# Norm rows behind the first FFN blocks, and a down projection with its load order written by hand

## The chip, the cores and the metric

The kernel runs on one core of a Trainium2 chip. The engines of the core work in parallel, each through its own instruction stream in order: TensorE (PE in the profile: matrix products into PSUM), VectorE (DVE), ScalarE (ACT), GpSimd (POOL) and SyncE (SP), which here does nothing but issue DMA transfers. They wait for each other through semaphores. The metric is the time of one execution on the device in microseconds. Before the change it is 1984.14 us, the median of three runs (1983.55 to 1985.42).

## The reference

One layer of a hybrid decoder for a prompt of 1024 tokens and 8 sample requests of 4 tokens each, so NT = 1056 tokens. Every sub-layer has a residual sum and an RMS norm ahead of it: a mixer (a gated MLP along the chunks beside a multi-head latent attention with a paged cache), a cross attention into a memory, and a convolutional FFN. Only the end of it matters here:

```python
o = einsum('nhtm,nmhd->nthd', p, mv); y = o @ w_mo          # memory cross-attention, out projection
x = x + y
h = rms_norm(x, g_ffn)                                      # x * rsqrt(mean(x*x) + eps) * g
gate, val = split(h @ w_up)                                 # 1024 -> 2 x 2816
conv = b_conv + sum(gpad[:, j:j+t] * w_conv[j] for j in range(3))
out = x + (silu(conv) * val) @ w_down                       # 2816 -> 1024
```

All is in 32-bit floating point with the precision that goes with it.

## The kernel before

Features lie on the 128 partitions and tokens along the free dimension. The 1056 tokens are two halves of HT = 528, each two columns of QT = 264. The 2816 features of the FFN are NF = 22 tiles of 128.

**Products.** Each operand is split into a rounded part hi and a rest lo (`split`, L186: ScalarE casts hi at L190, VectorE subtracts to lo at L191), and each product is three matmuls, hi by hi, hi by lo and lo by hi (`mm3`, L178 to L184). All products of the kernel therefore carry line 184 in the profile, and go by the names of what they write. A weight is loaded into `raw` (three buffers), and split into `hi` and `lo` (three buffers each); `stream` (L1302) does this for one tile of up to 8 blocks of 128 x 128.

**The memory attention's end** (`mem_attention`, L1524). `out` makes the output product in PSUM tiles named b, s and t in turn. VectorE adds each to the residual `res` (L1702), ScalarE multiplies by the gain into `y` (L1704) and squares for the norm (L1520), and GpSimd sums the squares into `ya`, the tile `acc` (L1521). `operands` (L1767) makes from y the seven operands of the FFN's blocks for each half (b11, b21, b22, t1, t3, t2, t4; sums by VectorE at L1775, splits at L190 and L191). The half's number is in the names: b110h is the hi part of b11 of half 0. The norm factor itself is not multiplied into the operands. `half_norm` (L1738) sums `ya` over the partitions by five matmuls and takes the inverse root in some dozen small VectorE operations (rqx, rqh, rqy, rqa, hr: L219 to L230). `half_row` (L1748) turns the 528 factors into a tile with the same row on each partition: five diagonal tiles by VectorE (`diag`, L1757), five matmuls with ones (sx, st: L1758), two copies by ScalarE (`row`, L1759). Both are called in the attention, ahead of the FFN, for half 0 and for half 1.

**The up projection** (`ffn_up`, L1830). Eleven pairs of feature tiles; for each pair four blocks: gate of half 0, gate of half 1, value of half 0, value of half 1. A `block` (L1843) is a 2 x 2 product by Winograd's form of Strassen's scheme, seven products in place of eight, in 84 matmuls: A (12), X twice (12 each), F (24), E (24), with sums by VectorE in between (a, z, zz) and results in G (gate) or C (value). The gate is multiplied by `row` (L1886), goes through the convolution (`cv`, L1893 to L1905), SiLU (L1906) and once more `row` (by GpSimd, L1907). The value block's C is multiplied in (L1923), and ScalarE's queue stores the result, the activation, in DRAM (`actd`, L1925). `weights` (L1794) makes the weights' sums on GpSimd (s12, s34: L1814 to L1818) and their splits.

**The down projection** (`ffn_down`, L1941). For each half it loads 22 activations (`araw`, a ring of four, L1952), splits them (`ah`, `al`, 27 buffers each), and for each of 8 output tiles m streams three weight tiles `w_down` of 8, 8 and 6 blocks and makes two columns `d` of 66 matmuls each. VectorE adds the residual (`yres`, loaded at L1967, added at L1968) and SP stores the output (`o_y`, L1969).

**Order.** The order of instructions on each engine is not that of the code: a scheduler with a timeline model of the chip orders them all, and adds the waits. Buffers come from pools with a fixed number per name; a tile waits until the last readers of the buffer's earlier tile are done. A pool that is opened where a closed one lay waits in the same way for that one's tiles. Only inside a manual section the named engines keep the order of the code.

Of the kernel before, what the change touches and what calls it, by code (L numbers as in the profile page):

```python
# [13 lines left out]
P = 128  # L14
# [8 lines left out]
FF, NF = 2816, 22  # L23

HT, QT = 528, 264
# [128 lines left out]
class Net:  # L154
# [1369 lines left out]
    def mem_attention(self, xh, xl, r3):  # L1524
        nc, tc, I, O = self.nc, self.tc, self.I, self.O
# [22 lines left out]
        w, st = {}, {}  # L1548
# [127 lines left out]
        self.pw, self.nw = self.open("pw", side="right"), 0  # L1676
        pc = self.open("pc", side="right")
        y1 = [self.t(pc, [P, 2, 2, HT], F32, f"y{d}") for d in range(2)]
        acc = self.t(pc, [P, 640], F32, "ya")
        pc0 = self.open("pc0", side="right")  # L1680
        nc.gpsimd.memset(acc[:, HT:], 0.0)

# [53 lines left out]
        return ops, rows, first  # L1736

    def half_norm(self, p, pp, acc):  # L1738

        nc = self.nc  # L1740
        st = self.t(pp, [P, 512], F32, "st", 1)
# [6 lines left out]
    def half_row(self, p, pp, r, row):  # L1748

        nc = self.nc  # L1750
        for a, z, tag in ((0, 4, "sx"), (4, 5, "st")):
            ps = self.t(pp, [P, 512], F32, tag, 1)
            n = min(HT, z * P) - a * P
            for i in range(a, z):
                w = min(P, HT - i * P)
                dg = self.t(p, [P, P], F32, "diag", 2)[:w, :w]
                nc.vector.tensor_scalar(dg, self.ident[:w, :w], r[:w, i : i + 1], None, ALU.mult)  # L1757
                nc.tensor.matmul(ps[:, (i - a) * P : (i - a) * P + w], self.ones[:w], dg, start=True, stop=True)  # L1758
            nc.scalar.copy(row[:, a * P : a * P + n], ps[:, :n])  # L1759
# [63 lines left out]
        w["a22"] = hi, lo  # L1823
        return w

    def ffn(self, ops, rows, w):
        self.ffn_up(ops, rows, w)
        self.ffn_down()

    def ffn_up(self, ops, rows, first):  # L1830

        nc, I, O = self.nc, self.I, self.O
        p = self.open("pf")
# [33 lines left out]
        def gate(w, fs, h, prev):  # L1867
# [73 lines left out]
    def ffn_down(self):  # L1941

        nc, I, O = self.nc, self.I, self.O
        p = self.open("pd", side="right")
        pp = self.open("psd", space=PSUM)
        parts = ((0, 8), (8, 16), (16, 22))
        for h in range(2):
            o = h * HT
            act = []
            for k in range(NF):  # L1950
                raw = self.t(p, [P, HT], F32, "araw", 4)
                nc.sync.dma_start(raw, self.act_dram[:, k, o : o + HT])  # L1952
                hi, lo = (self.t(p, [P, HT], FR, x, 27) for x in ("ah", "al"))
                self.split(hi, lo, raw)
                act.append((hi, lo))
            for m in range(8):
                ps = [self.t(pp, [P, 512], F32, "d", 6)[:, :QT] for c in range(2)]
                for a, z in parts:
                    w = self.stream(I["w_down"][m, :, a:z], z - a)
                    for c in range(2):  # L1960
                        t = slice(c * QT, c * QT + QT)
                        self.mm3(ps[c], [(w[0][:, k], w[1][:, k]) for k in range(z - a)],
                                 [(act[k][0][:, t], act[k][1][:, t]) for k in range(a, z)], first=a == 0, last=z == NF)
                for c in range(2):
                    t = slice(o + c * QT, o + c * QT + QT)
                    res = self.t(p, [P, QT], F32, "yres", 4)
                    nc.sync.dma_start(res, self.y_dram[:, m, t])  # L1967
                    nc.vector.tensor_tensor(res, ps[c], res, ALU.add)  # L1968
                    nc.sync.dma_start(O["o_y"][m, :, t], res)  # L1969
        self.close("psd")  # L1970
        self.close("pd")


def build(tc, I, O, stop=99, tap=None):
# [35 lines left out]
        N.close(x)  # L2010
    if done(5):
        return
    ops, rows, w = N.mem_attention(xh, xl, r3)
    if done(6):
        return
    N.ffn(ops, rows, w)
    for name in reversed(list(N.pools)):
        N.close(name)

# [30 lines left out]
```

## Time and profile before

| what | value |
|---|---|
| median of three runs | 1984.14 us |
| profiled execution | 1984.73 us |
| its span, first to last instruction | 1983.0 us |
| mean granted TensorE clock | 0.978 of full |
| TensorE busy | 1881.5 us, 95% |
| VectorE, ScalarE, GpSimd busy | 1363.9, 899.7, 707.1 us |
| first and last product of the up projection | 1256.25 and 1705.5 us |
| last product of the down projection | 1979.2 us |

The profile is that of one execution. Its page gives each engine's busy time, a chain of work that ended last (followed back from the last instruction, at each step to what released it), the costliest groups of instructions, and the DMA issues with their median time from issue to landing. Answers of the trace give single instructions with start and duration, what an engine waited for, and tables by stretches of time. PE means matmuls, SPq and ACTq the queues on which SP and ScalarE issue transfers. "x24" is a count.

### The profile page before, as it was taken

The numbers are of one execution on the slowest core, as the hardware profiler recorded it, in microseconds if no ns is written. First come the engines' busy times: TensorE is split into PE (matmuls) and PEld (weight loads), VectorE is DVE, ScalarE is ACT, GpSimd is POOL, SyncE is SP. The second block draws the span as 40 slices with busy tenths as digits, with TensorE's granted clock in tenths as the row PEclk, the third lists the DMA queues.
The fourth block names the chain that finished last, engine by engine and source line by source line (L and its number), as shares of the span: only waits on it lengthen the run. The fifth ranks groups of instructions, "written<-read, shape, count | busy, mean of one in ns | idle before, by whom it ended". The sixth has DMA issues, their size and how long they took to land.

```text
span 1983.0 us, 40178 instructions
## 1 busy us (share of the span) xinstructions
PE 1881.5 (95%) x14556; PEld 1768.9 (89%) x14556; DVE 1363.9 (69%) x2988; ACT 899.7 (45%) x1878; POOL 707.1 (36%) x811
## 2 busy tenths in 40 slices
PE   6999799999999999999999987799999999899999
PEld 5999777768898899888899976799999999899999
DVE  7865867766777766776645659788888888642521
ACT  6334676665555555555432546333333323331411
POOL 5231402003544444444032026377677776100000
PEclk9999899999999999999999999799999999899999
DMA  5101100207765566653653065022222222664642
GB/s 200 50 5 60 45 1 1 74 2 205 214 178 172 157 178 178 177 168 128 187 171 130 22 210 161 22 87 81 82 69 74 86 91 72 183 193 124 201 126 65
DMA packets 130312, 229.42 MB, mean 116 GB/s; under 512 B 20449, under 2 KB 86850, under 8 KB 130114
## 3 DMA queue, kind: packets, MB, share of 16 engines
q1 hardware_dynamic: 122914, 213.91, 36.1%
q10 hardware_dynamic: 7200, 12.95, 1.7%
q8 instruction: 115, 1.88, 0.4%
q14 instruction: 83, 0.68, 0.1%
HBM read 195.13 MB, written 31.66 MB: 114 GB/s over the span
## 4 chain that ended last, share of the span: by engine, by line
PE 69%; DVE 9%; issue 4%; DMA 3%; POOL 1%; ACT 1%; SPq 0%; POOLq 0%; DVEq 0%; ACTq 0%
PE s L184 15%; PE d L184 12%; PE b L184 7%; PE X L184 6%; PE F L184 6%; PE E L184 6%; PE A L184 3%; PE o L847 2%; PE tp L834 2%; DMA araw<-actd 1%; PE tp L184 1%; PE o L1277 1%; DVE mx L1228 1%; PE tp L789 1%; DVE y L1775 1%
## 5 line engine op out<-in xcount | busy, mean ns | idle before, releaser
L184 PE MATMUL s<-w2h,ch 128*128 128x288 f32 (+1 forms) x1024 | 306.7, 299 | 0.0
L184 PE MATMUL s<-w2h,cl 128*128 128x288 f32 (+1 forms) x1024 | 295.6, 289 | 2.1 <-POOL cl L1164 1.3
L184 PE MATMUL s<-w2l,ch 128*128 128x288 f32 (+1 forms) x1024 | 295.4, 288 | 0.0
L184 PEld LDWEIGHTS s<-w2h,ch 128*128 128x128 f32 x1024 | 193.3, 189 | 19.1 <-issue 13.6
L184 PE MATMUL d<-ah,hi 128*128 128x264 f32 x704 | 200.7, 288 | 9.0 <-ACT ah L190 9.0
L184 PE MATMUL d<-al,hi 128*128 128x264 f32 x704 | 201.2, 287 | 0.0
L184 PE MATMUL d<-ah,lo 128*128 128x264 f32 x704 | 201.2, 287 | 0.0
L184 PEld LDWEIGHTS s<-w2h,cl 128*128 128x128 f32 x1024 | 193.1, 189 | 2.8 <-POOL cl L1164 1.6
L184 PEld LDWEIGHTS s<-w2l,ch 128*128 128x128 f32 x1024 | 193.5, 189 | 0.0
L1207 DVE TENSOR_REDUCE ss<-sq 128x16 f32<-128x1024 f32 x128 | 155.4, 1214 | 50.0 <-ACT sq L1204 49.8
L191 DVE TENSOR_TENSOR lo<-raw,hi 128x1024 fp32r<-128x1024 f32 (+1 forms) x71 | 82.8, 1169 | 134.8 <-ACT hi L190 134.8
L190 ACT CAST hi<-raw 128x1024 fp32r<-128x1024 f32 (+1 forms) x71 | 70.9, 999 | 184.7 <-PE d L184 152.8
L1164 POOL TENSOR_TENSOR cl<-cT,ch 128x512 fp32r<-128x512 f32 x64 | 83.5, 1304 | 170.3 <-ACT ch L1160 151.5
L184 PEld LDWEIGHTS d<-ah,hi 128*128 128x128 f32 x704 | 133.9, 191 | 9.9 <-ACT ah L190 9.9
L184 PEld LDWEIGHTS d<-al,hi 128*128 128x128 f32 x704 | 134.3, 191 | 0.5 <-DVE al L191 0.5
L184 PEld LDWEIGHTS d<-ah,lo 128*128 128x128 f32 x704 | 134.1, 191 | 0.0
L1204 ACT ACTIVATE sq<-s 128x512 f32<-128x512 f32 x128 | 76.5, 598 | 92.2 <-PE s L184 92.2
L1201 ACT ACTIVATE sq<-s 128x512 f32<-128x512 f32 x128 | 76.6, 599 | 85.3 <-PE s L184 85.0
L184 PE MATMUL mm<-whi,xh 128*128 128x256 f32 (+3 forms) x288 | 84.7, 296 | 12.7 <-ACT xh L194 11.2
L184 PE MATMUL mm<-whi,xl 128*128 128x256 f32 (+3 forms) x288 | 82.6, 298 | 6.5 <-DVE xl L197 6.4
L1521 POOL TENSOR_TENSOR acc<-acc,sqx 128x384 f32<-128x384 f32 (+1 forms) x42 | 46.2, 1101 | 111.7 <-ACT sqx L1520 110.7
L184 PE MATMUL mm<-wlo,xh 128*128 128x256 f32 (+3 forms) x288 | 84.3, 294 | 0.0
(672 smaller groups left out, 6316.8 us busy)
## 6 DMA issues: line engine op xcount, KB each, us to landing
cT<-cT SPq DMA_DIRECT2D x256, 160.0 KB, 2.6
ck<-ck SPq DMA_DIRECT2D x256, 144.0 KB, 3.2
raw<-w_up SPq DMA_DIRECT2D x44, 512.0 KB, 3.6
raw<-w_down SPq DMA_DIRECT2D x32, 512.0 KB, 3.8
actd<-cv ACTq DMA_DIRECT2D x44, 264.0 KB, 2.3
araw<-actd SPq DMA_DIRECT2D x44, 264.0 KB, 4.0
raw<-w_down SPq DMA_DIRECT2D x16, 384.0 KB, 3.2
res<-res SPq DMA_DIRECT2D x16, 264.0 KB, 2.8
```

The lines of the kernel that those rows point to most:

```text
L184: self.nc.tensor.matmul(out, l, r, start=first and i == 0, stop=last and i == len(seq) - 1)
L190: {"act": nc.scalar.copy, "pool": nc.gpsimd.tensor_copy, "dve": nc.vector.tensor_copy}[eng](hi, src)
L191: low = lambda: nc.vector.tensor_tensor(lo, src, hi, ALU.subtract)
L789: nc.tensor.transpose(tp[:, j * P : j * P + P], s[x, g * 4 + j][:, h % 4], self.ident)
L834: nc.tensor.transpose(tp[:, z * P : z * P + P], u[e][:, jj * P : jj * P + P], self.ident)
L847: nc.tensor.matmul(u["o"][jj * 64 : jj * 64 + 64, c], s["v"][:, j + jj, h % 4], th[:, jj * 256 : jj * 256 + c.stop - c.start], start=j == ...
L1164: (nc.vector if k else nc.gpsimd).tensor_tensor(d["l"][:, k], src[k], d["h"][:, k], ALU.subtract)
L1201: nc.scalar.activation(sq[:, 0], ps[:, :, n0 : n0 + 256], AF.Square)
L1204: nc.scalar.activation(sq[:, 1], pt.rearrange("p (e d) -> p e d", e=2), AF.Square)
L1207: yield lambda: nc.vector.tensor_reduce(s["ss"][:, g0 : g0 + 2].rearrange("p e (z h) -> p z e h", z=2), sq.rearrange("p z e (h d) -> p z e ...
L1228: nc.vector.tensor_reduce(s["m"][:, z], S[:, g0:g1].rearrange("p g m -> p m g"), AX.X, ALU.max)
L1521: nc.gpsimd.tensor_tensor(acc, acc, sq, ALU.add)
```

## The change

There are three parts. The norms move: `ya`, the norm factors and the diagonal tiles lie in the pool `pw`, which stays open through the FFN, and `half_norm` and `half_row` take their PSUM from the caller. Half 0's `half_norm` stays in the attention; its row, and half 1's norm and row, are made in `ffn_up` behind the first gate block of the half, with PSUM from the ring "A" of the blocks. The value's C shares the ring of two buffers of G. And `ffn_down` is written anew: hi and lo of an activation share one tile "a" with 27 buffers, and 16 tiles that are never used are taken ahead of the first, so that the first eleven activations get buffers 16 to 26, which lie where half 0's operands b11 to t2 were, while the others follow from buffer 0 on. The order of SP is that of the code: four activations, the first three weight tiles, 18 activations, and then for each m two `yres`, the next m's weight tiles and the two stores of the m before; half 1's activations 0 to 4 follow the products of m = 6 of half 0, and 5 to 21 the stores that stand in half 1's m = 0.

```diff
-        acc = self.t(pc, [P, 640], F32, "ya")
+        acc = self.t(self.pw, [P, 640], F32, "ya")
...
-        norms = [self.half_norm(pc, pp, acc)]
+        norms = [self.half_norm(self.pw, self.t(pp, [P, 512], F32, "st", 1), acc)]
...
-        self.half_row(pc, pp, norms[0], rows[0])
...
-        self.half_row(pc, pp, self.half_norm(pc, pp, acc), rows[1])
...
+        def norm(h, new):
+            if h:
+                norms.append(self.half_norm(self.pw, new(), acc))
+            self.half_row(self.pw, new, norms[h], rows[h])
...
             block(w, ops[h], place)
+            if fs[0] == 0:
+                norm(h, lambda: self.t(pp, [P, 512], F32, "A", 2))
...
-            C = self.t(p, [P, 4 * QT], F32, "C")
+            C = self.t(p, [P, 2, HT + 2], F32, "G", 2).rearrange("p e n -> p (e n)")[:, : 4 * QT]
...
+        def raws(m):
+            out = []
+            for a, z in parts:
+                out.append(self.t(self.wr, [P, 8, P], F32, "raw")[:, : z - a])
+                nc.sync.dma_start(out[-1], I["w_down"][m, :, a:z])
+            return out
+        def acts(h, ks):
+            for k in ks:
                 raw = self.t(p, [P, HT], F32, "araw", 4)
+                nc.sync.dma_start(raw, self.act_dram[:, k, h * HT : h * HT + HT])
+                a = self.t(p, [P, 2, HT], FR, "a", 27)
+                self.split(a[:, 0], a[:, 1], raw)
+                act[h].append((a[:, 0], a[:, 1]))
+        def store(h, m, ps):
+            for c in range(2):
+                t = slice(h * HT + c * QT, h * HT + c * QT + QT)
+                nc.vector.tensor_tensor(res[h, m][c], ps[c], res[h, m][c], ALU.add)
+                nc.sync.dma_start(O["o_y"][m, :, t], res[h, m][c])
+        for _ in range(16):
+            self.t(p, [P, 2, HT], FR, "a", 27)
+        act, res = [[], []], {}
+        with self.tc.manual_schedule(engines={mybir.EngineType.SP}):
+            acts(0, range(4))
+            raw = raws(0)
+            acts(0, range(4, NF))
+            old = None
+            for h in range(2):
+                for m in range(8):
+                    res[h, m] = []
                     for c in range(2):
+                        res[h, m].append(self.t(p, [P, QT], F32, "yres", 4))
+                        nc.sync.dma_start(res[h, m][c], self.y_dram[:, m, h * HT + c * QT : h * HT + c * QT + QT])
+                    w = [self.stream(None, z - a, raw=r) for (a, z), r in zip(parts, raw)]
+                    if h + m < 8:
+                        raw = raws((m + 1) % 8)
+                    if old:
+                        store(*old)
+                    if (h, m) == (1, 0):
+                        acts(1, range(5, NF))
+                    ps = [self.t(pp, [P, 512], F32, "d", 6)[:, :QT] for c in range(2)]
+                    for (a, z), x in zip(parts, w):
+                        for c in range(2):
...
+                    if (h, m) == (0, 6):
+                        acts(1, range(5))
+                    old = h, m, ps
+            store(*old)
```

More of the change, by code (lines that the diff above doesn't have):

```diff
@@ L1732, in mem_attention, with half_norm @@
             self.operands(y1[d], d, ops[1], self.FORMS[3:])
-        self.half_row(pc, pp, self.half_norm(pc, pp, acc), rows[1])
         self.close("psa")
         self.close("pc")
-        return ops, rows, first
-    def half_norm(self, p, pp, acc):
+        def norm(h, new):
+            if h:
+                norms.append(self.half_norm(self.pw, new(), acc))
+            self.half_row(self.pw, new, norms[h], rows[h])
+        return ops, rows, norm, first
+    def half_norm(self, p, st, acc):
         nc = self.nc
-        st = self.t(pp, [P, 512], F32, "st", 1)
         for i in range(5):
@@ L1746, in half_norm, with half_row @@
         return r
-    def half_row(self, p, pp, r, row):
+    def half_row(self, p, new, r, row):
         nc = self.nc
-        for a, z, tag in ((0, 4, "sx"), (4, 5, "st")):
-            ps = self.t(pp, [P, 512], F32, tag, 1)
+        for a, z in ((0, 4), (4, 5)):
+            ps = new()
             n = min(HT, z * P) - a * P
@@ L1824, in weights, with ffn, ffn_up @@
         return w
-    def ffn(self, ops, rows, w):
-        self.ffn_up(ops, rows, w)
+    def ffn(self, *a):
+        self.ffn_up(*a)
         self.ffn_down()
-    def ffn_up(self, ops, rows, first):
+    def ffn_up(self, ops, rows, norm, first):
         nc, I, O = self.nc, self.I, self.O
@@ L1946, in ffn_down @@
         parts = ((0, 8), (8, 16), (16, 22))
[L1947 to L1950, printed above, removed]
-                raw = self.t(p, [P, HT], F32, "araw", 4)
[L1952 to L1959, printed above, removed]
-                    for c in range(2):
[L1961 to L1969, printed above, removed]
@@ new lines, in store @@
+        def store(h, m, ps):
[14 more added lines that the diff above has]
+                    res[h, m] = []
+                    for c in range(2):
+                        res[h, m].append(self.t(p, [P, QT], F32, "yres", 4))
[10 more added lines that the diff above has]
+                        for c in range(2):
+                            t = slice(c * QT, c * QT + QT)
+                            self.mm3(ps[c], [(x[0][:, k], x[1][:, k]) for k in range(z - a)],
+                                     [(act[h][k][0][:, t], act[h][k][1][:, t]) for k in range(a, z)], first=a == 0, last=z == NF)
+                    if (h, m) == (0, 6):
+                        acts(1, range(5))
+                    old = h, m, ps
+            store(*old)
@@ L2012, in build @@
         return
-    ops, rows, w = N.mem_attention(xh, xl, r3)
+    ffn = N.mem_attention(xh, xl, r3)
     if done(6):
         return
-    N.ffn(ops, rows, w)
+    N.ffn(*ffn)
     for name in reversed(list(N.pools)):
```

## The prediction

> **What bounds the kernel now.** I read the page's busy shares and chain first, then the chain of waits around the two places that the change touches, then the timelines of single engines there. TensorE is busy almost the whole span and heads the chain, so time can only come out of stretches in which it stands still or runs at half clock.
>
> ```profile
> PE 1881.5 (95%) x14556; PEld 1768.9 (89%) x14556; DVE 1363.9 (69%) x2988; ACT 899.7 (45%) x1878; POOL 707.1 (36%) x811
> PE 69%; DVE 9%; issue 4%; DMA 3%; POOL 1%; ACT 1%; SPq 0%; POOLq 0%; DVEq 0%; ACTq 0%
> ```
>
> The FFN's up projection has no such stretch: in its stage TensorE is busy 448.75 of 449.00 us at full clock (columns: busy time and count by engine, granted clock, DMA share, GB/s).
>
> ```profile
> 1256.00:1705.00 449.00, 448.75 (x3681) 448.75 (x3682) 374.50 (x480) 153.59 (x199) 301.46 (x230) 1.00 0.24 77
> ```
>
> The stretches lie before and behind it. The first, from the chain (start, duration, what):
>
> ```profile
> 1225.65 1.64 PE b L184 x11
> 1234.35 0.34 DVE res L1702
> 1234.69 3.21 DVE diag L1757 x2
> 1250.12 0.62 DVE t41l L191
> 1250.73 0.09 DVE rqy L222
> 1253.08 2.39 PE sx L1758 x8
> 1255.49 0.72 ACT row L1759 x2
> 1256.25 3.01 PE A L184 x12
> 1259.26 3.17 PE X L184 x24
> 1278.48 1.47 PE A L184 x12
> 1288.69 1.46 PE A L184 x12
> ```
>
> The last output product of the memory attention ends at 1227.3. VectorE then makes half 1's operands (to 1250.7) and the norm, and the first FFN matmul starts at 1256.25, at half clock (3.01 us for an A that takes 1.46 later). A block is 10.2 us (1278.48 to 1288.69). The second stretch is the change to the down projection:
>
> ```profile
> 1704.17 1.34 PE E L184 x11
> 1705.54 0.84 ACT hi L190
> 1706.40 0.97 DVE lo L191
> 1709.19 6.62 DMA araw<-actd
> 1722.73 2.74 DMA araw<-actd
> 1735.99 4.07 DMA araw<-actd
> 1740.77 238.41 PE d L184 x1957
> 1979.21 0.43 DVE yres L1968
> ```
>
> From 1740.77 the products run without a gap: 238.41/1957 = 0.1218 us each. All 2112 (2 halves, 8 m, 22 k, 2 columns, 3 terms) are 257.3 us; the rest, 155, would be 18.9 us, and 1705.5 to 1740.77 is 35.3. So this transition costs 16.4 us. At the switch of halves nothing is lost now.
>
> **The change part by part.**
>
> *Norm moved behind the first gate blocks.* TensorE's next work after the last b is now block A of half 0, which needs only its weights. Its X writes PSUM that the attention's output products used, free behind VectorE's last add into res (1234.69); X, X, F, E of half 0 then run with nothing further from VectorE. That they may run at half clock costs nothing, since they end long before the next wait does. The row of half 0 (5 diag and matmuls) lies in the idle time that follows. Half 1's X needs z of half 0's block, which stands in VectorE's queue behind all the operand work, so it starts at about 1251, not before t41l has ended (1250.74). X, X, F and E are 8.8 us (10.2 less an A), so half 1's gate block ends at about 1260.3. Before it ended at 1278.48: a gain of 18.2 us up to here, if nothing else is late.
>
> What is late next is half 1's norm: 5 matmuls on acc, some 13 small VectorE operations (rqx to hr), 5 diag, 5 matmuls, two copies by ScalarE. It now takes PSUM from block A's ring of two buffers, so the A's of the value blocks wait for it. TensorE has X, X, F, E of value h0 as cover: 8.8 us, to 1269.1. In the trace the part from rqy at 1250.73 to the row's end at 1256.2 takes 5.5 us, and with the operations before it some 6. It can begin behind the last G of half 1's gate block, about 1261, and would end at 1267: hidden, but only while GpSimd is still, as it was there. These rows show the same operations beside a running GpSimd:
>
> ```profile
> 1217.05 1.29 DVE L222 TENSOR_SCALAR rqy<-rqy 128x5 int32<-128x5 int32 x1
> 1220.42 1.09 DVE L227 TENSOR_TENSOR rqa<-rqy 128x5 f32<-128x5 f32 x1
> 1223.02 0.47 DVE L1757 TENSOR_SCALAR diag<-ident,hr 128x128 f32<-128x128 f32 x2
> 1234.62 3.29 DVE L1757 TENSOR_SCALAR diag<-ident,hr 128x128 f32<-128x128 f32 x2
> 1251.05 0.17 DVE L228 TENSOR_TENSOR rqa<-rqa,rqh 128x5 f32<-128x5 f32 x1
> 1261.07 0.43 DVE L1852 TENSOR_TENSOR z<-X,a 128x264 f32<-128x264 f32 x1 [2.66 <-PE X L184]
> ```
>
> ```profile
> 1216.91 1.41 POOL L1521 TENSOR_TENSOR ya<-ya,sqx 128x528 f32<-128x528 f32 x1 [2.75 <-ACT sqx L1520]
> 1233.95 2.61 POOL L1803 TENSOR_TENSOR lo<-s,hi 128x1024 fp32r<-128x1024 f32 x1 [0.16 <-ACT hi L1802]
> 1275.19 2.98 POOL L1803 TENSOR_TENSOR lo<-s,hi 128x1024 fp32r<-128x1024 f32 x1 [0.18 <-ACT hi L1802]
> 1284.51 2.31 POOL L1815 TENSOR_TENSOR s<-s,raw 128x512 f32<-128x512 f32 x1
> ```
>
> A 0.17 us operation took 1.29 and 1.09 in the length of a GpSimd add, and two diag took 3.29, not 0.47, beside a lo. From 1275.19 to 1286.8 GpSimd runs without a pause on the weights of the value blocks and on cv times row: 11.6 us, and it now has this work while the norm runs. How much of it falls between the norm's operations is not in the trace. Ends: none (gain 18.2) and all (chain ends at 1278.6, stall 9.5, gain 8.7). I take two thirds, GpSimd's busy share in the stage (301.46 of 449.00): 7.8 us, chain end 1274.8, stall 5.7; and 1.4 us for what then stands behind the late A (the copy of A, z and a further VectorE operation). Gain 11.
>
> The Trainium skill (SBUF — State Buffer, "Who interferes with whom") says that VectorE operations with two SBUF inputs, and tensor_scalar in a 2-port mode, are fully blocked while GpSimd reads SBUF, and those with one input from PSUM are not. These rows agree: z from PSUM is 0.43 us. The page speaks for the end "all" where GpSimd is never still; by it alone the gain would be 8.7.
>
> *ya, hr, rq and diag in another pool; C in G's ring.* Nothing: value h0's C takes the buffer of half 0's G, whose last reader (the two copied columns) is half 1's gate, 10 us earlier; the Memset of the next G goes later on GpSimd. If that cover were gone, VectorE's first write of C would wait behind one GpSimd operation at most, 3 us (the lo of 2.98); with 10 us of cover in a stage without gaps I take 0.
>
> *FFN to down projection.* The first four activations are loaded ahead of FFN's end, into the space of half 0's operands. But their split stands on ScalarE behind the last two stores of act, which wait for VectorE's last product:
>
> ```profile
> 1709.37 0.81 ACTq L1925 DMA_DIRECT2D actd<-cv  x2
> 1711.25 0.63 ACT L190 CAST ah<-araw 128x528 fp32r<-128x528 f32 x1 [4.88 <-DMA araw<-actd]
> 1720.63 1.33 ACT L190 CAST ah<-araw 128x528 fp32r<-128x528 f32 x2 [4.17 <-DMA araw<-actd]
> 1744.20 0.63 ACT L190 CAST ah<-araw 128x528 fp32r<-128x528 f32 x1 [0.93 <-DMA araw<-actd]
> ```
>
> ```profile
> raw<-w_down SPq DMA_DIRECT2D x32, 512.0 KB, 3.8
> actd<-cv ACTq DMA_DIRECT2D x44, 264.0 KB, 2.3
> araw<-actd SPq DMA_DIRECT2D x44, 264.0 KB, 4.0
> ```
>
> With T = 1705.5 the stores are issued by T + 2.5 to 4.7, four splits of 0.63 and the weights' hi of 0.84 to 1.05 follow, and the first d starts at about T + 6, as before (1711.9). Act 4 comes earlier: its load is ordered behind the landing of the last store (T + 4.7 or so), so with 2.7 to 4.1 us to land it is split from T + 9.5, not T + 15.1 (1720.63). From there 18 activations go through a ring of four raw buffers: load, 0.63 hi, 0.7 lo, next load. The trace has five such rounds from 1720.63 to 1744.20: 4.7 us each; the quickest that the rows give is 2.74 + 1.36 = 4.1, the longest seen 5.5. With rounds of L, m = 0 ends at T + 9.5 + 4 L + 2.7 (two hi, a lo, six products). Its weights and those of m = 1 are ordered by hand behind all the activations on the SP queue, so nothing of m = 1 fills the gaps, as it did before. L = 4.7 gives T + 31.0, of which 132 products are 16.1 us: 14.9 lost, against 16.4. Gain 1.5, with 3.9 at 4.1 and -1.7 at 5.5.
>
> *Switch of halves.* Only activations 0 to 4 of half 1 have free buffers early. Number 5 and on are issued on SP behind the third raw of the next m, which waits for the last weights' lo (T0 + 0.84 + 0.97, T0 the end of half 0), and behind two stores of o_y (0.43 us each on VectorE, and their issue): T0 + 3.1. Landing at 2.7 to 4.0 puts the first split at T0 + 6.6, then four rounds, the last with a hi, a lo and six products: m = 0 ends at T0 + 8.7 + 4 L. TensorE has 132 products (16.1 us) and 42 of the next m that its order lets run ahead (5.1 us). L = 4.7 gives 27.5 - 21.2 = 6.3 lost; 3.9 at 4.1, 9.5 at 5.5. Before, nothing. The other m are fed in time: a raw is released one m (16.1 us) ahead of its use, and load, hi and lo are 3.8 + 1.05 + 1.2. The queue behind the waiting loads (yres and the raws of m = 2) has all of m = 1 as cover.
>
> **Sum.** 11 + 1.5 - 6.3 = 6.2 us. The profiled execution took 1984.73, 0.6 over the median of the runs, so 1978.5.
>
> **The rivals.** (a) The norm is wholly hidden, GpSimd's work falling elsewhere. For: the small operations take 0.17 each where it is still. Against: the POOL rows. Gain 18.2 + 1.5 - 6.3 = 13.4: 1971.3. (b) The norm pays for all of GpSimd's work, by the blocked pairs of rows above: 8.7 - 1.4 + 1.5 - 6.3 = 2.5: 1982.2, no measurable change. (c) Slower: the rounds of four loads are the bound at both places and are longer than before, since more loads of other kinds share the queue. Each us of L costs 8 us (four rounds, twice). L = 5.5 gives 1984.9 or so; from L = 5.9 the kernel is slower by over 0.2% (4 us, about what a measurement tells from no change), and 6.3 gives 1991. For: the landing of 6.62 us at 1709.19, where stores and loads met; against: the longest round was 5.5 and the five average 4.7. (d) The early activations bring nothing, or less: if act 4 comes no earlier than before, m = 0 ends 5.6 us later, for 1984: the same as (b) to the eye, told apart by act 4's time.
>
> **How the numbers follow.** My sum 0.30, (a) 0.14, (b) 0.16, (c) 0.26, (d) 0.14. Faster holds (a) and my sum; no change holds (b) and half of (d), slower (c) and the other half, since a first round that slips may slip further. That is 0.44, 0.23, 0.33. The range runs from (a) to (c): 1971 to 1991; that of my sum alone is 1975 to 1982.
>
> **What the changed profile would show.** TensorE starts A of the first block within 2 us of the last b; its half 1 gate block ends near 1260, and there is a wait on ACT row (PE A) of 4 to 8 us behind value h0's E; pair 0 is complete near 1288, not 1299. Behind FFN the first d stays at T + 6, act 4's split comes at T + 9.5, and the d group starts being gapless near T + 31. A new wait on act 5 to 21 stands at the switch of halves, 6 us in all. I am wrong if the diag or rq operations show no stretching, if half 1's X does not wait for z, or if a round differs much from 4.7 us.

## The result and the profile after

The changed kernel takes 1989.04 us (median of 13 runs, 1986.04 to 1992.48) and the kernel before, on the same chip, 1982.74 (13 runs): the ratio is 1.0034, with a 95% interval of 1.0025 to 1.0042. The change costs 6.3 us, where I had forecast a gain of 6.2. The time lies inside my range; the sign is wrong.

The profiled execution of the changed kernel took 1988.78 us. I cut both executions at the same four events: the end of the attention's last b, the last E of the up projection, the 1056th product of the down projection (the end of half 0) and its last product. The loss is what a stretch takes beside its 1056 products of 0.1218 us, 128.6 us.

| stretch | before | changed |
|---|---|---|
| last b to last E | 1227.4 to 1707.1: 479.7 | 1225.0 to 1700.3: 475.3 |
| last E to end of half 0, loss | 14.8 | 17.8 |
| half 1, loss | 0.1 | 8.0 |

So the norm's move gains 4.4 and the new down projection loses 10.9 (3.0 and 7.9), 6.5 in all. (The 2.4 us by which the changed kernel's last b was earlier come from ahead of the change and count for neither.) These are rows in which TensorE waits (what waited, for what, us in total, times, longest), without those inside the attention: the longest of the kernel before in the window from 1100 to 1320, then the changed kernel's in the same window, then those behind it:

```profile
PE sx L1758 <- DVE diag L1757: 17.7, 3, 8.9
...
PE X L184 <- DVE res L1702: 6.0, 1, 6.0
PE F L184 <- DVE G L1880: 4.3, 1, 4.3
PE A L1762 <- DVE diag L1761: 3.6, 1, 3.6
PE A L184 <- ACT row L1763: 0.2, 1, 0.2
...
PE d L184 <- ACT hi L190: 9.4, 2, 6.3
PE d L184 <- ACT a L190: 4.8, 4, 4.1
```

Of the 17.7 us that TensorE waited for `diag` before, 3.6 are left, for half 0's row; the change means that. Waits of X and F on VectorE have come in their place. The chain of the changed kernel around it:

```profile
1223.28 1.62 PE b L184 x11
1249.08 3.76 PE X L184 x22
1269.26 5.62 PE F L184 x24
1279.02 0.59 ACT row L1763
1279.65 4.88 PE A L184 x36
```

And VectorE's timeline there (start, duration, operation), which holds the reason:

```profile
1257.19 2.48 DVE L1900 SCALAR_TENSOR_TENSOR cv<-G,cols,cv 128x528 f32<-128x528 f32 x2
1259.60 0.42 DVE L1856 TENSOR_TENSOR z<-X,a 128x264 f32<-128x264 f32 x1
1260.28 3.93 DVE L1901 SCALAR_TENSOR_TENSOR cv<-G,cols,cv 128x528 f32<-128x528 f32 x2
1264.13 0.69 DVE L1864 TENSOR_TENSOR zz<-F,z 128x528 f32<-128x528 f32 x1
1264.75 1.21 DVE L1807 TENSOR_TENSOR lo<-raw,hi 128x1024 fp32r<-128x1024 f32 x1
1265.88 2.89 DVE L1826 TENSOR_TENSOR l<-raw,h 128x512 fp32r<-128x512 f32 x1
1268.69 0.42 DVE L1880 TENSOR_TENSOR G<-F,zz 128x264 f32<-128x264 f32 x1
1269.65 0.15 DVE L219 TENSOR_SCALAR rqx<-A 128x5 f32<-128x5 f32 x1
1273.21 0.48 DVE L1761 TENSOR_SCALAR diag<-ident,hr 128x128 f32<-128x128 f32 x2
```

F of the next block has one PSUM buffer; its last reader, the add at 1268.69, stands in VectorE's queue behind half 0's convolution, a lo and an l. The norm of half 1 stands behind it and starts at 1269.65, not one gate block behind the operands as I had it.

In the down projection, the chain shows two places (the third column names the work; SPq is the issue on SP's queue):

```profile
1726.27 5.14 DMA raw<-w_down
1731.51 1.05 ACT hi L190
1732.61 1.22 PE d L184 x4
...
1846.80 0.84 ACT hi L190
1849.03 0.43 SPq L1973
1851.02 4.80 DMA araw<-actd
1870.55 29.51 PE d L184 x239
```

The first is m = 1 of half 0, waiting for its weights, which SP issued behind all the activations. The second is the switch: 1846.8 is the end of half 0, and the load of activation 5 follows the stores of o_y.

### The profile page after: what moved, and what is told of

Read it like the earlier page. It is cut to its first block, busy times and chain, and to the rows that moved or that the text cites. A ratio compares the mean times of both kernels' runs of the same rounds, so it can differ in the third digit from the quotient of the medians.

```text
span 1986.7 us, 40183 instructions
## 1 busy us (share of the span) xinstructions
PE 1891.5 (95%) x14556; PEld 1775.8 (89%) x14556; DVE 1368.8 (69%) x2988; ACT 900.9 (45%) x1878; POOL 704.8 (35%) x811
## 4 chain that ended last, share of the span: by engine, by line
PE 67%; DVE 9%; issue 5%; DMA 4%; ACT 2%; POOL 1%; SPq 0%; ACTq 0%; DVEq 0%; POOLq 0%
PE s L184 16%; PE d L184 11%; PE b L184 7%; PE F L184 6%; PE X L184 6%; PE E L184 6%; PE A L184 3%; PE o L847 2%; PE tp L834 2%; DMA araw<-actd 1%; PE tp L184 1%; PE o L1277 1%; DVE y L1779 1%; DVE mx L1228 1%; PE tp L789 1%
## 5 line engine op out<-in xcount | busy, mean ns | idle before, releaser
L184 PE MATMUL d<-a,hi 128*128 128x264 f32 x1408 | 265.6, 290 | 14.6 <-ACT hi L190 9.4
L184 PEld LDWEIGHTS d<-a,hi 128*128 128x128 f32 x1408 | 222.1, 192 | 18.6 <-ACT hi L190 9.8
L184 PE MATMUL d<-a,lo 128*128 128x264 f32 x704 | 201.0, 287 | 0.0
L184 PEld LDWEIGHTS d<-a,lo 128*128 128x128 f32 x704 | 134.5, 192 | 0.9 <-DVE lo L191 0.9
L1807 POOL TENSOR_TENSOR lo<-s,hi 128x1024 fp32r<-128x1024 f32 x22 | 69.3, 3152 | 44.6 <-ACT hi L1806 44.6
L1160 ACT CAST ch<-cT 128x512 fp32r<-128x512 f32 x128 | 73.6, 629 | 3.0 <-DMA cT<-cT 3.0
```

The source lines that it names most:

```text
L184: self.nc.tensor.matmul(out, l, r, start=first and i == 0, stop=last and i == len(seq) - 1)
L1160: nc.scalar.copy(d["h"][:, k], src[k])
L1807: eng.tensor_tensor(lo, src, hi, ALU.subtract)
```

## The experiments

A number behind a run is the median of its runs and its ratio to the kernel before, run on the same chip, with the 95% interval; a run without an interval had one execution. "Stage" is the time from the last b to the last E, "loss" what the down projection holds beside its 257.3 us of products. The text set off under each edit is what was expected before the run.

**The parts apart** (e1_norm_only and e2_down_only). First, the norm's move and C's ring with the old `ffn_down`; second, the new `ffn_down` with the old norm.

Against the changed kernel these are:

```diff
-        def raws(m):
...
-        with self.tc.manual_schedule(engines={mybir.EngineType.SP}):
...
+        for h in range(2):
+            o = h * HT
+            act = []
+            for k in range(NF):
+                raw = self.t(p, [P, HT], F32, "araw", 4)
```

```diff
-            if fs[0] == 0:
-                norm(h, lambda: self.t(pp, [P, 512], F32, "A", 2))
...
-            C = self.t(p, [P, 2, HT + 2], F32, "G", 2).rearrange("p e n -> p (e n)")[:, : 4 * QT]
+            C = self.t(p, [P, 4 * QT], F32, "C")
...
+        self.half_row(pc, pp, self.half_norm(pc, pp, acc), rows[1])
```

> Norm rows moved and C in G's ring, the down projection as before. From the last b of the attention to the last E of the up projection the changed kernel took 475.4 us and the one before 478.2 (1224.90 to 1700.32, 1227.29 to 1705.51). Theory (the parts act apart): this stage again 475.4, the down projection as before, so 2.8 us faster than before, about 1980. Rival (the parts help each other, the early activations for instance take the stage's DMA time): the stage comes out more than 1 us off 475.4.

> The new down projection alone, norms as before. In the changed kernel the transition from the last E to the switch of halves held 17.9 us beside its products (146.45 less 1056 x 0.1218) and the second half 8.0 (136.59 less 128.6); before it was 16.4 and 0. Theory (apart): the stage up to the last E stays 478.2, and both losses come back, 17.9 and 8.0: 9.4 us slower than before, about 1992. Rival (the early activations need the norm's move to gain anything): the transition is over 19 us.

The 478.2 in them, the 16.4 of the prediction and the 1705.5 in the table of the kernel before rest on a misreading that I found afterwards: the chain leaves E at 1705.51, since what released the next step was an earlier product; E itself goes on to 1707.1, so the stage before is 479.7 and the transition 14.8. With the norm's move alone: 1976.7, ratio 0.9969 (0.9957 to 0.9981), stage 475.2, loss 11.4. With the down projection alone: 1994.4, ratio 1.0069 (1.0043 to 1.0095), stage 480.1, loss 26.6 (18.7 and 8.0). One part is faster, the other slower, and each stage comes back as in the changed kernel. What I had not expected is the loss of 11.4 with code that held 14.8 before; it is taken up below.

**What the norm costs** (e3_no_norm). As e1_norm_only, with the norm left out: the two rows are constants.

```diff
             block(w, ops[h], place)
-            if fs[0] == 0:
-                norm(h, lambda: self.t(pp, [P, 512], F32, "A", 2))
...
+        for h in range(2):
+            nc.gpsimd.memset(rows[h], 1.0)
```

> As e1_norm_only, but the two rows are constants of 1, set early: half 1's norm, both rows' diagonals, products and copies are left out, and the output is not the reference's. The first half 1 gate block ended 35.9 us behind the last b in the changed kernel, and 42 blocks of 10.17 us were left: 462.9 us if nothing stalls behind it; it took 475.4. Theory (VectorE's backlog beside GpSimd holds F, whose PSUM has one buffer; the norm's own work is the smaller part): a wait of F on VectorE stays, and the stage takes 467 to 472. Rival (the norm's chain and its place in block A's ring cost the 12.5 us): no wait is left, and the stage takes 462 to 465.

The stage is 464.4. The rival holds in its time, though waits of F of 1.2 and 0.5 us are left: the norm costs 10.8 us where it stands, and this includes what it makes late. Some of TensorE's waits in this kernel:

```profile
PE X L184 <- DVE z L1858: 2.7, 1, 2.7
PE F L184 <- DVE G L1924: 1.2, 1, 1.2
PE F L184 <- DVE G L1882: 0.5, 1, 0.5
```

Without the norm the scheduler also puts the add that frees F ahead of lo and l, so the wait of F is nearly gone, and I could not say from this run whether the norm's own work or that order cost the 10.8.

**The factors early, the row late** (e4_early_norm, on e1_norm_only).

```diff
+        norms.append(self.half_norm(self.pw, self.t(pp, [P, 512], F32, "st", 1), acc))
         self.close("psa")
...
-            if h:
-                norms.append(self.half_norm(self.pw, new(), acc))
```

> As e1_norm_only, but half 1's norm factors (five products and 13 small VectorE operations) are made at the attention's end, behind the operands, and only its row (diagonals, products, copies) behind the first gate block. In e1_norm_only the stage from the last b to the last E took 475.2 us, without any norm 464.4: the norm costs 10.8 where it stands. Theory (the factors come late, since they stand behind the gate block in VectorE's order, and all that follows waits): the stage falls to 467 to 472, with half 1's X up to 3 us later. Rival (the diagonals and the row's products in block A's ring cost it): it stays at 474 or more.

1978.1, ratio 0.998 (0.997 to 0.9989); stage 477.3, loss 10.9. This does not separate the two, since it moved something else: the norm's tile in the attention's PSUM is now read at 1244.2, and the first block's A waited for that.

```profile
PE st L1746 <- POOL ya L1521: 11.0, 1, 11.0
PE A L184 <- DVE rqx L219: 7.0, 1, 7.0
PE F L184 <- DVE G L1879: 1.6, 1, 1.6
```

It shows something of its own: counted from the last b, half 0's A came 20 us and its X 16 us later than in e1_norm_only, and the stage is only 2.1 us longer. This run also spares the late chain, worth 5.3 us by e16_row_only below. By an estimate from these two differences the early block is worth some 7 us, and not the 18 that its start suggests.

**GpSimd quiet** (e8_quiet_pool, on e1_norm_only). For the first pair's value weights no sums and no lo are made on GpSimd; ScalarE copies in their place.

```diff
-            eng.tensor_tensor(lo, src, hi, ALU.subtract)
+            if quiet and eng is nc.gpsimd:
+                nc.scalar.copy(lo, src)
+            else:
+                eng.tensor_tensor(lo, src, hi, ALU.subtract)
...
+        if quiet:
+            add = lambda out, x, y, op: nc.scalar.copy(out, x)
...
-            w = self.weights(NF + fs[0], NF + fs[1], p)
+            w = self.weights(NF + fs[0], NF + fs[1], p, quiet=q == 0)
```

> As e1_norm_only, but for the first pair's value weights GpSimd makes nothing: the sums become copies by ScalarE and the last lo a copy, so these weights are wrong and the output is not the reference's. It takes some 9.2 us of GpSimd away between 1257 and 1271. Theory (VectorE is blocked by GpSimd there: two cv took 3.93 and an l 2.89 us): F's wait of 4.3 us goes and the stage takes 470 to 472 instead of 475.2. Rival (the order of VectorE's queue and the norm's late start cost it, with GpSimd or without): 474 or more.

The stage is 469.7, 5.5 us less, but for the most part not where I had put it: the theory's time came, its mechanism only in part. Of these operations the four sums ran at 1226 to 1239, and only the lo stood behind 1257. In the changed kernel it is this row, beside the two cv of 3.93 us:

```profile
1260.80 2.85 POOL L1807 TENSOR_TENSOR lo<-s,hi 128x1024 fp32r<-128x1024 f32 x1
```

The sums that I had seen behind 1257 belong to the next pair, and they are still made here. X of half 0 waits 3.3 instead of 6.0 us, and half 1's X starts 20.2 us behind the last b instead of 23.8: 3.6 of the 5.5 us lie in half 1's operands, which VectorE makes while GpSimd makes these sums. Behind half 1's first block 1.9 us are gained; the wait of F fell only from 4.3 to 3.7.

```profile
PE F L184 <- DVE G L1885: 3.7, 1, 3.7
PE X L184 <- DVE res L1702: 3.3, 1, 3.3
```

**The order of VectorE's queue** (e11_post_late). The first pair's convolution of half 0 stands behind half 1's block and norm in the code (half 1's first two columns are copied before half 0's row is multiplied in, so part of the convolution differs from the reference). This and the next run have the tiles of the changed kernel and the scheduler's order on SP (e9_space_only, below; stage 473.9).

```diff
             block(w, ops[h], place)
-            if fs[0] == 0:
-                norm(h, lambda: self.t(pp, [P, 512], F32, "A", 2))
+            return G
+
+        def post(fs, h, G):
             row = rows[h].unsqueeze(1).broadcast_to([P, 2, HT])
...
+            if q == 0:
+                Gs = [gate(w, fs, 0, None)]
+                norm(0, new)
+                Gs.append(gate(w, fs, 1, Gs[0]))
+                norm(1, new)
+                cvs = [post(fs, h, Gs[h]) for h in range(2)]
```

> As e9_space_only, but the first pair's convolution of half 0 stands behind half 1's gate block and norm in the code; on VectorE the write that frees F (G from F and zz) then comes ahead of a weights' lo and l (1.2 and 2.9 us in the changed kernel) instead of behind them. Theory (that place in VectorE's queue made the 4.3 us wait of F and the half clock behind it): no wait of F over 1 us, and the stage falls from 473.9 to 467 to 470. Rival (the norm's chain, which starts no earlier, sets the end): the wait of F goes but A's wait on the row takes its place, and the stage stays at 472 or more.

1976.0, ratio 0.9958 (0.9942 to 0.9974); stage 473.6. The add that frees F is now ahead of lo and l, F waits 1.1 us instead of 4.3, and the stage is the same. These are the waits of this run, and what TensorE did behind half 1's row, first here and then in e9_space_only (start, duration):

```profile
PE A L1762 <- DVE diag L1761: 5.4, 2, 3.9
PE F L184 <- DVE G L1880: 1.1, 1, 1.1
...
1276.02 7.40 PE A L184 x36
...
1277.86 4.88 PE A L184 x36
```

3.9 of the 5.4 us are half 0's row, as before; half 1's row waits 1.6. These products of A start 50.4 us behind the last b here and 53.3 in e9_space_only. But the granted clock is 0.53 from 1275 to 1282, behind the pauses ahead of the row, and 1.00 in e9_space_only from 1277 to 1283, so they take 2.5 us longer. The stage stays, as the rival has it; only a part of that is the wait that it names, and the clock is the larger part. The wait of F in the changed kernel was the first wait one sees, and taking it away alone gains nothing.

**The norm ahead of half 1's block** (e10_norm_ahead).

```diff
+            if fs[0] == 0 and h:
+                norm(h, lambda: self.t(pp, [P, 512], F32, "A", 2))
             block(w, ops[h], place)
-            if fs[0] == 0:
+            if fs[0] == 0 and not h:
                 norm(h, lambda: self.t(pp, [P, 512], F32, "A", 2))
```

> As e9_space_only, but half 1's norm and row stand ahead of its first gate block in the code, so in the stretch in which TensorE waits for half 1's operands. e9_space_only took 473.9 us from the last b to the last E; without a norm it was 464.4. Theory (the norm's chain costs as much as it is late behind the gate block): 466 to 471 here. Rival (wherever the chain stands behind the operands in VectorE's queue, it and the blocked VectorE operations cost the same): 473 or more.

1982.2, ratio 1.0002 (0.9991 to 1.0012); stage 480.7. All that the move gained is gone, and the rival holds: TensorE waits 12.2 us for the diagonals, 4.0 of them for half 0's row and 8.2 for half 1's, behind X, F and E of half 1's first block and ahead of its A.

**The row without the chain** (e16_row_only, on e1_norm_only). Half 1's row is made from half 0's factors.

```diff
-            if h:
-                norms.append(self.half_norm(self.pw, new(), acc))
-            self.half_row(self.pw, new, norms[h], rows[h])
+            self.half_row(self.pw, new, norms[0], rows[h])
```

> As e1_norm_only, but half 1's row is made from half 0's factors: its products on acc and its 13 small VectorE operations are left out, its diagonals, products and copies stay behind the gate block, and the output is not the reference's. With the norm this stage took 475.2 us, without any row 464.4. Theory (the chain of small operations, begun late, costs it): 465 to 469. Rival (the row's diagonals and products in block A's ring cost it): 472 or more.

469.9, between the two. By these differences the chain of small operations with its products costs 5.3 of the 10.8 us and the row itself the other 5.5. The split is rough: here too the scheduler put the add that frees F ahead of lo and l, and F waits 1.8 us instead of 4.3.

```profile
PE A L1760 <- DVE diag L1759: 5.1, 2, 3.6
PE F L184 <- DVE G L1878: 1.8, 1, 1.8
```

**The order on SP at the switch** (e5_switch).

```diff
+                    if (h, m) == (1, 0):
+                        acts(1, range(5, NF))
                     if h + m < 8:
                         raw = raws((m + 1) % 8)
                     if old:
                         store(*old)
-                    if (h, m) == (1, 0):
-                        acts(1, range(5, NF))
```

> The changed kernel, but half 1's activations 5 to 21 are issued on SP ahead of the raw weights and the stores that stand in half 1's m = 0, so that they follow the release of their buffers during half 0's m = 7. Theory (the place on the queue costs the 8.0 us): the second half's loss falls to between 0 and 3, the whole to about 1982 to 1984. Rival (the ring of four raw buffers and its rounds of 4.7 us cost it, wherever they stand): the loss falls by no more than the 3 us between T0 and the first issue, to 5 or more, and the whole stays at 1986 or above.

1982.6, ratio 1.0003 (0.9993 to 1.0012). The loss of half 1 is 0.8 us, not 8.0; TensorE waits 0.3 us in all behind 1760. The place on the queue was the cause, and the same ring of four buffers costs next to nothing when its loads follow the buffers' release through m = 7. (Its transition took 19.8, against 17.8 and 18.7 in the two others with that order. m = 1 began at half clock in all three: the granted clock was 0.72 from 1732 to 1738 in the changed kernel and 0.51 from 1731 to 1738 here, which is 1.7 against some 3 us.)

**The weights of m = 1 ahead of the last activations** (e7_both_down). As above, and:

```diff
-            acts(0, range(4, NF))
+            acts(0, range(4, 14))
...
                         store(*old)
+                    if (h, m) == (0, 0):
+                        acts(0, range(14, NF))
```

> As e5_switch, and also half 0's activations 14 to 21 are issued behind the raw weights of m = 1. e5_switch held 20.5 us beside its products; in the changed kernel m = 1 began at 1732.6 since its weights landed at 1731.4, and the last activation was split by 1728.7. Theory (the weights of m = 1 behind all activations cost 3 us): the loss falls to 16 to 18, the whole to about 1979 to 1980. Rival (the rounds of the ring set it, and the weights' 1.3 MB only takes time from them): no change against e5_switch within 1 us.

1979.6, ratio 0.9986 (0.9976 to 0.9995); loss 16.0, of which 15.5 at the transition. That is 4.3 less than in the run above, but only 2.3 less than in the changed kernel, whose transition has the same order; the medians of the two runs differ by 3. The theory holds with some 3 us.

**The last stores off ScalarE** (e13_store_pool). As above, with the last two stores of act on GpSimd's queue.

```diff
-                nc.scalar.dma_start(self.act_dram[:, f, h * HT : h * HT + HT], cv[:, e])
+                q = nc.gpsimd if fs[1] == NF - 1 and h else nc.scalar
+                q.dma_start(self.act_dram[:, f, h * HT : h * HT + HT], cv[:, e])
```

> As e7_both_down, but the last two stores of act are issued by GpSimd instead of ScalarE, so that ScalarE's first four splits no longer stand behind them. Theory (the prediction's step: the early activations wait for these stores): the hi of activations 0 to 3 are made ahead of the last E, activation 4 is split 1.5 us or more earlier than in e7_both_down (T + 8.2 in the changed kernel), and the loss of 16.0 falls to 14 to 15. Rival (VectorE's lo stands behind the last product as well, so nothing is gained): no change within 0.7 us.

1979.8, ratio 0.9989 (0.9976 to 1.0003); transition loss 15.8 against 15.5. Activation 4 is split 7.2 us behind the last E instead of 8.3, and nothing comes of it. ScalarE's first split moved from 3.05 to 2.2 us behind the last E, no further: it waits for VectorE's last product itself, stores or not.

```profile
ACT a L190 <- DVE cv L1929: 10.5, 1, 10.5
```

The rival holds, and of the theory's 1.5 us or more for activation 4 there is some 1.

**The order left to the scheduler** (e9_space_only). The changed kernel, tiles and early buffers kept, without the section that fixes SP's order.

```diff
-        with self.tc.manual_schedule(engines={mybir.EngineType.SP}):
+        if True:
```

> The changed kernel without the section that keeps SP's order as written: tiles, rings and early buffers as changed, the order of SP by the scheduler. The down projection held 25.7 us beside its products in the changed kernel (283.0 less 257.3), 14.8 before (272.1 less 257.3, the last E ending at 1707.1). Theory (the hand-given order costs it, at the switch and by the late weights of m = 1): the loss falls to 10 to 15 and the whole to 1976 to 1981. Rival (the shared tile and the early buffers themselves cost some of it): it stays over 18.

1974.6, ratio 0.9966 (0.9953 to 0.9978): the loss is 13.0 (12.8 and 0.3) and the stage 473.9. It is faster than both kernels. The theory holds; what made the changed kernel slower is the hand-given order. (Two runs above have the same code for the down projection: e10_norm_ahead held 13.7 and e11_post_late 14.0.) It is no faster than e1_norm_only beyond the noise (ratio 0.9969), where the old `ffn_down` held 11.4: no run here shows a gain from the shared tile and the early buffers themselves.

**The kernel before again, and C alone** (e12_before_again without an edit, e14_c_ring).

```diff
-            C = self.t(p, [P, 4 * QT], F32, "C")
+            C = self.t(p, [P, 2, HT + 2], F32, "G", 2).rearrange("p e n -> p (e n)")[:, : 4 * QT]
```

> The kernel before once more, for the size of what differs between two profiled executions of the same program. Both theories: the stage from the last b to the last E within 0.5 us of 479.7. The down projection held 14.8 us in the first profile and 11.4 in e1_norm_only, with the same code: if these are two draws of the DMA's times, it may come out anywhere between 11 and 15; if the up projection's tiles make the difference, it comes out at 14 to 15.5.

> The kernel before with one change: the value's C shares G's ring. The down projection's code held 14.8 and 14.6 us beside its products in the kernel before, and 11.4, 10.9, 11.6 and 11.3 in the four kernels with the norm's edits. Theory (C's own tile lies where the down projection's first loads go, and they wait for it): the loss falls to 11 to 12 and the whole by some 3 us, to 1979 to 1980. Rival (the moved norm tiles or the up projection's order make the difference): it stays at 14 to 15.

The kernel before again has a stage of 480.4 and a loss of 14.6 (479.7 and 14.8 the first time), so two executions of the same program differ by 0.7 us in the stage and 0.2 in the loss, and the five kernels with the norm's edits and the old `ffn_down` held 10.9 to 11.8: a loss of 11.4 is not a draw. With C's edit alone the loss is 13.0 and the ratio 0.9992 (0.9981 to 1.0003): half of the 3.3 us, and neither theory. The rest stays open.

## Why the prediction was wrong

By its own steps, in us (a minus is a loss):

| step | predicted | measured |
|---|---|---|
| norm behind the gate blocks | +11 | +4.4 |
| FFN to down projection | +1.5 | -3.0 |
| switch of halves | -6.3 | -7.9 |
| sum | +6.2 | -6.5 |

Of the 12.7 us between the two sums, 6.6 lie in the norm, 4.5 in the change to the down projection and 1.6 at the switch. The first two are steps that failed, one by one below. That the time lies in the range is luck: the range's upper end came from a rival whose mechanism was not the one that ran.

**The norm.** That A follows the last b at once, that X waits for VectorE's last add, and that half 1's X stands behind all operands was right: it started 23.7 us behind the last b, as forecast (1251 less 1227.3). The block behind it then took 12.2 us (to 1260.9), not 8.8. I had let its A run ahead, but A's ring held half 0's row; and X ran in part at half clock. So the gain at that point was 15.2, not 18.2. Behind it I had 7.1 us of loss (5.7 and 1.4), of which GpSimd's work was the main part. The trace gives, from 1260.75: 1.0 for the products on ya, 4.3 of wait for F, 2.5 for F at half clock (5.4 instead of 2.9, from its start to E's), 1.4 in E for the row's products and 0.7 until the row is copied: 9.9 of the 10.8 that were lost. The step that failed is "it can begin behind the last G of half 1's gate block, about 1261": it began at 1269.65, counted from the last b 11 us late, since VectorE's queue held the convolution, lo and l before it. I had priced the wait of a small operation for GpSimd; the chain of small operations was hardly stretched (one of 1.26 us), which I had named as a sign of being wrong, while the large ones ahead of it were, 3.93 and 2.89. Nor was there a wait of A on the row of 4 to 8 us; it was 0.2, and F waited in its place. Without the chain half of the loss goes, with the lo on GpSimd taken away 1.9 us, and with the add for F moved up none. So no single wait binds. That it is the whole stretch of VectorE's work between the gate block and the row is what these runs suggest; none of them takes away that stretch alone.

The Trainium skill (SBUF — State Buffer, "Who interferes with whom") says that a VectorE operation with two SBUF inputs is blocked by a GpSimd operation that reads SBUF. These runs agree: without GpSimd's sums the operands ahead of half 1's X came 3.6 us earlier, and z at 1259.60, with one input from PSUM, takes 0.42 beside such a sum. (The z that the prediction shows, 0.43 at 1261.07, says nothing on it: GpSimd was idle there, from 1251.1 to 1270.4.)

```profile
1259.19 1.65 POOL L1819 TENSOR_TENSOR s<-s,raw 128x512 f32<-128x512 f32 x1
```

**FFN to down projection.** Two terms were off. The transition before costs 14.8, not 16.4, since I took the place where the chain leaves E for E's end. And "m = 0 ends at T + 31.0" was near enough for the activations, with rounds of 4.4 us and an end at T + 29.2 (13.1 us beside its products, T being 1700.3 here), but the stretch ends with the weights of m = 1: issued behind the 18 activations and two yres, they landed in 5.14 us, at 1731.4. TensorE waited 3.1 us for them, and began m = 1 at half clock, worth another 1.7. This is the step that failed: I had noted the order and that nothing of m = 1 fills the gaps, and not asked when m = 1 could start. The run with those weights moved ahead gives some 3 us back.

```profile
1705.25 19.82 SPq L1964 DMA_DIRECT2D araw<-actd  x18
1726.27 1.39 SPq L1958 DMA_DIRECT2D raw<-w_down  x3
...
1849.03 0.90 SPq L1973 DMA_DIRECT2D o_y<-yres  x2
1849.97 18.96 SPq L1964 DMA_DIRECT2D araw<-actd  x17
```

That ScalarE's first splits are late was right, and its reason only half: the stores stand ahead of them, but without these they wait for VectorE all the same.

**The switch.** The mechanism and the place were right (issue at T0 + 3.1; measured 1849.97, T0 + 3.2), the size 6.3 against 7.9. Behind TensorE's gap of 4.1 us (1850.5 to 1854.6) the granted clock was 0.63 from 1856 to 1860, worth some 1.5 us, which I had not counted.

**The rivals.** I gave the norm that pays for all of GpSimd's work a gain of 8.7, less 1.4; it gained 4.4. The slower rival put the loss on the length of a round, 5.9 us or more; the rounds were 4.4 at the transition and 4.7 at the switch, and it was the place on the queue. Its sign was right, its mechanism was not. Nor was it the rival of the early activations: act 4 was split at T + 8.2, earlier than I had it.

## What to carry to other kernels

A wait that is moved behind other work is hidden only if the engine that must end it is free then: count that engine's whole queue between the two places, and not the moved operations alone. In an order written by hand, ask of each queue what the next stage needs first: here one group of weights behind 18 loads and one group of loads behind two stores cost more than the norm's move gained, and the same tiles with a computed order gained 0.34%, no more than the norm's move alone (0.31%). And the end of a piece of the chain is the place where the chain leaves a group, not the end of the group; a stage is cut at the group's last instruction.

## What the runs showed of the hardware

TensorE's clock fell within or just behind pauses of 3 to 4 us. The changed kernel's windows (busy time and count by engine, then granted clock, DMA share, GB/s):

```profile
1266.00:1268.00 2.00, 0.00 (x0) 0.00 (x0) 2.00 (x1) 0.00 (x0) 2.00 (x1) 1.00 0.00 0
1268.00:1270.00 2.00, 0.74 (x3) 0.77 (x4) 1.97 (x6) 0.00 (x0) 2.00 (x3) 0.61 0.25 16
1270.00:1272.00 2.00, 2.00 (x11) 2.00 (x10) 1.84 (x6) 0.00 (x0) 1.14 (x1) 0.50 0.63 246
1732.00:1738.00 6.00, 5.36 (x30) 5.05 (x31) 3.32 (x3) 2.34 (x3) 0.00 (x0) 0.72 0.60 180
1856.00:1860.00 4.00, 4.00 (x24) 4.00 (x24) 2.61 (x4) 2.38 (x4) 0.00 (x0) 0.63 0.74 227
```

The last product ahead of the first gap ended at 1264.9; by the 0.61 of the window from 1268 the clock fell at about 1268.4, 3.5 us later. In the kernel before TensorE's last products ahead of the pause are four of half 0's row, which end at 1227.8; by the 0.58 of the window below the clock fell at about 1232.3, 4.5 us later:

```profile
1227.23 0.61 PE L1758 MATMUL sx<-diag,ones 128*128 128x128 f32 x4
...
1232.00:1234.00 2.00, 0.00 (x0) 0.00 (x0) 2.00 (x3) 1.87 (x3) 1.36 (x2) 0.58 0.33 127
```

A pause of 4 us can thus cost more than its own length: F took 5.4 instead of 2.9 us. The Trainium skill (TensorE: Matmul & The Clock Gate, "Part 1: The HAM clock gate") says that the window is about 3.4 us long and runs free, and shows a fall 5.2 us behind the last matmul; 3.5 and 4.5 us here agree with a window whose start is not tied to the work.
